# One transpose for both key blocks of a sliding-window attention, and its scaling as one operation a step later

## The chip, the cores and the metric

The kernel runs on one core of a Trainium2 chip. The metric is the device time of one launch in microseconds, of the one core that takes part. Engines: TensorE (PE) multiplies and transposes into PSUM; VectorE (DVE) and ScalarE (ACT) read and write SBUF and PSUM; GpSimd (POOL) works on SBUF; SyncE (SP) issues loads. Each engine works its own queue in order.

## The reference, cut to what matters

Two decoder layers for a prompt of 1024 tokens and a group of 8 samples: layer 0 mixes tokens by gated linear attention, layer 1 by attention over a sliding window, each followed by a squared-ReLU MLP. The change lies in the prompt's attention of layer 1:

```python
def sink_probs(scores, mask, sinks):
    s = jnp.where(mask, scores, -jnp.inf)
    sk = sinks.astype(jnp.float32).reshape(SWA_KV_HEADS, SWA_GROUP)[:, :, None, None]
    m = jnp.maximum(jnp.max(s, axis=-1, keepdims=True), sk)
    p = jnp.exp(s - m)
    return p / (jnp.sum(p, axis=-1, keepdims=True) + jnp.exp(sk - m))

def swa_attend_prompt(q, k, v, sinks):          # 8 blocks of 128 queries
    kk, vv = with_prev(k), with_prev(v)         # keys of the block before, and of the block
    scores = jnp.einsum('bnqkgd,bnskd->bnkgqs', qb, kk).astype(jnp.float32) * (SWA_HEAD_DIM ** -0.5)
    diff = SWA_BLOCK + i - j                    # i: query 0..127, j: key 0..255
    mask = (diff >= 0) & (diff <= SWA_WINDOW) & (key_pos >= 0)
    p = sink_probs(scores, mask[None, :, None, None], sinks)
    o = jnp.einsum('bnkgqs,bnskd->bqnkgd', p.astype(vv.dtype), vv)
```

Window and block are both 128. So query i of a block sees the keys j >= i of the block before and the keys j <= i of its own: the two triangles meet only on the diagonal, where both count. There are 16 query heads of 64 columns over 4 key heads.

## The kernel before

The tokens go in two groups: A is tokens 0 to 511 and the 8 samples, B is tokens 512 to 1023. All linear layers are computed in float32r with a split of each operand into a high and a low part: `split_w` makes `wh` (ACT cast, L201) and `wl` (DVE subtraction, L202) of a weight, `split` the same of an activation (L304, L305), and `mms` issues three matmuls for each tile (L225, L227, L229). The linear layers are cut into jobs, one for each 128 output columns; each job's weights are split while the job before it runs.

The attention is a generator in the background. After each linear job `tick` adds its time to a credit, and while the credit is positive the generator is advanced to its next `yield`, which costs PACE. So attention work of one group is strewn between linear jobs of the other: A's attention beside B's MLP of layer 0, B's beside A's MLP of layer 1. A scheduler then puts each engine's instructions into their final order; `keep_in_program_order` holds an instruction at its place.

`swa_attention` works on 16 units for each group, key head j by query block n, each with 4 query heads (two `m`, two `i`). One step is two halves with a `yield` after each:

- first half: `turn` of unit i-2, which transposes the factors on PE into `ppt` (L1041), once for each key block `kk`, and splits them out of PSUM into `ph` (ACT) and `pl` (DVE); then `softmax` of unit i-1;
- second half: `values` of unit i-2 (L1052, L1053, then `ot`, `of` and a split into the input of the output projection) and `queries` of unit i, a split of `q` into `qs` (ACT L998, L999, DVE L1000, L1001).

`softmax` computes the scores into `psc` (L1012), adds the mask and takes the maximum (L1018, DVE, out of PSUM into `pb`), combines it with the sink (L1022 to L1024), takes the exponential with its sum (ACT, L1026), makes the reciprocal of the whole sum (L1029, L1030), and scales the factors by it with one DVE operation for each head (L1032). This is done for each `m` apart. Units with n = 0 of group A have no block before them (`first`): 4 units with one key block, 28 with two.

Other work on the engines in these stretches: `yf` is the sum of the down projections (DVE, L836, reads PSUM), `hl` the low half of the MLP's hidden values (L305). The rotary embedding `rope`, which runs ahead of each group's attention, is the one place where POOL computes: `qsw` times a sine table (L901), beside a DVE product of the same size (L902).

Of the kernel before, what the change touches and what calls it, by code (L numbers as in the profile page):

```python
# [12 lines left out]
F32 = mybir.dt.float32  # L13
# [7 lines left out]
P = 128  # L21
# [14 lines left out]
PB = 4  # L36
# [32 lines left out]
def tile_hybrid_gla_swa_decoder(  # L69
# [885 lines left out]
    def swa_cache_out(sp, g):  # L955
# [9 lines left out]
    def swa_attention(S, sp, g):  # L965
# [25 lines left out]
        def queries(u):  # L991
# [8 lines left out]
            nc.vector.tensor_tensor(out=qs[dn, 0], in0=q[up], in1=r(qs[up, 0]), op=ALU.subtract)  # L1000
            nc.vector.tensor_tensor(out=qs[up, 1], in0=q[dn], in1=r(qs[dn, 1]), op=ALU.subtract)  # L1001

        def softmax(u):
            kh, kl = keys[u.j]
            k0, n = u.k0, u.n
            u.p = []
            for m in range(2):
# [6 lines left out]
                pb = sp.tile([P, 2, 256], F32, tag="pb", name="pb", bufs=PB)  # L1014
                st = sp.tile([P, 8], F32, tag="st", name="st", bufs=4)
                mx = sp.tile([P, 2], F32, tag="mx", name="mx", bufs=4)
                for i in range(2):
                    nc.vector.tensor_tensor_reduce(out=pb[:, i, k0:], in0=ps[:, i, k0:], in1=S.mask[:, k0:],  # L1018
                                                   scale=1.0, scalar=-3e38, op0=ALU.add, op1=ALU.max,
                                                   accum_out=mx[:, i:i + 1])  # L1020
                sk = S.sink[:, 4 * u.j + 2 * m:4 * u.j + 2 * m + 2]
                nc.vector.tensor_tensor(out=mx, in0=mx, in1=sk, op=ALU.max)  # L1022
                nc.vector.tensor_tensor(out=st[:, 0:2], in0=sk, in1=mx, op=ALU.subtract)
                nc.vector.tensor_scalar_mul(mx, mx, -1.0)  # L1024
                for i in range(2):
                    nc.scalar.activation(out=pb[:, i, k0:], in_=pb[:, i, k0:], func=AF.Exp, bias=mx[:, i:i + 1],  # L1026
                                         accum_out=st[:, 2 + i:3 + i])
                nc.scalar.activation(out=st[:, 0:2], in_=st[:, 0:2], func=AF.Exp)
                nc.vector.tensor_tensor(out=st[:, 4:6], in0=st[:, 0:2], in1=st[:, 2:4], op=ALU.add)  # L1029
                nc.vector.reciprocal(out=st[:, 4:6], in_=st[:, 4:6])  # L1030
                for i in range(2):
                    nc.vector.tensor_scalar_mul(pb[:, i, k0:], pb[:, i, k0:], st[:, 4 + i:5 + i])  # L1032
                u.p.append(pb)
# [435 lines left out]
```

## Time and profile before

| | |
|---|---|
| runs shown | 2276.53, 2277.38, 2277.74 us; median 2277.38 |
| the profiled execution | 2277.55 us, of which the profile's span is 2275.7 |
| PE | busy 2247.7 us, 14612 matmuls and transposes |
| DVE | busy 1470.3 us, 3166 instructions |
| ACT | busy 1218.5 us, 2575 instructions |
| POOL | busy 88.7 us, 133 instructions |
| granted TensorE clock | 0.998 of full speed |
| A's attention, B's attention | first scores at 1044 and 1545, last value products at 1244 and 1780 us |

The span is the time between the first and the last recorded instruction; some 1.85 us of the execution lie around it. A row of the profile gives line, engine and operation, what is written and read, how often, and the mean duration in ns; matmuls are pipelined, so their durations overlap, and what one costs PE is the time from its start to the next start.

### The profile page before, as it was taken

The numbers are of one execution on the slowest core, as the hardware profiler recorded it, in microseconds if no ns is written. First come the engines' busy times: TensorE is split into PE (matmuls) and PEld (weight loads), VectorE is DVE, ScalarE is ACT, GpSimd is POOL, SyncE is SP. The second block draws the span as 40 slices with busy tenths as digits, with TensorE's granted clock in tenths as the row PEclk, the third lists the DMA queues.
The fourth block names the chain that finished last, engine by engine and source line by source line (L and its number), as shares of the span: only waits on it lengthen the run. The fifth ranks groups of instructions, "written<-read, shape, count | busy, mean of one in ns | idle before, by whom it ended". The sixth has DMA issues, their size and how long they took to land.

```text
span 2275.7 us, 39181 instructions
## 1 busy us (share of the span) xinstructions
PE 2247.7 (99%) x14612; PEld 2043.4 (90%) x14612; DVE 1470.3 (65%) x3166; ACT 1218.5 (54%) x2575; POOL 88.7 (4%) x133
## 2 busy tenths in 40 slices
PE   7999999999999999999999999999999999999998
PEld 7998889889999998998888989989999899888886
DVE  5578665676644457666887487658888478544445
ACT  5556644475434445535766456536766456443433
POOL 4010000100000000120000000020000000000000
PEclk9999999999999999999999999999999999999999
DMA  5444322445333335343222354432222354533322
GB/s 169 130 117 118 98 74 77 126 137 157 94 93 90 93 93 170 95 115 88 80 86 78 99 161 135 128 106 85 75 79 76 93 162 127 162 120 93 102 86 77
DMA packets 389183, 247.25 MB, mean 109 GB/s; under 512 B 17816, under 2 KB 368120, under 8 KB 388192
## 3 DMA queue, kind: packets, MB, share of 16 engines
q1 hardware_dynamic: 360736, 196.85, 29.9%
q10 hardware_dynamic: 24000, 25.58, 3.8%
q0 software_dynamic: 4256, 22.31, 2.9%
q8 instruction: 115, 1.88, 0.3%
q14 instruction: 76, 0.62, 0.1%
HBM read 221.19 MB, written 24.25 MB: 108 GB/s over the span
## 4 chain that ended last, share of the span: by engine, by line
PE 92%; DVE 3%; DMA 2%; ACT 1%; issue 1%; ACTq 0%; POOL 0%; DVEq 0%; SPq 0%; POOLq 0%
PE psl L225 25%; PE psl L227 25%; PE psl L229 25%; PE psd L1291 2%; PE psd L1293 2%; PE psd L1292 2%; PE psc L1012 1%; PE ppt L1041 1%; PE pO L727 1%; PE pO L725 1%; PE po L1052 1%; PE po L1053 1%; PE pP L700 1%; DMA wst<-in_swa_w_qkv_dram 0%; DVE wl L202 0%
## 5 line engine op out<-in xcount | busy, mean ns | idle before, releaser
L225 PE MATMUL psl<-xh,wh 128*128 128x512 f32 (+2 forms) x2784 | 890.8, 320 | 0.6 <-ACT sr L554 0.4
L227 PE MATMUL psl<-xl,wh 128*128 128x512 f32 (+2 forms) x2784 | 886.8, 319 | 0.1
L229 PE MATMUL psl<-xh,wl 128*128 128x512 f32 (+2 forms) x2784 | 886.1, 318 | 0.6 <-DVE wl L202 0.5
L201 ACT CAST wh<-wst 128x512 fp32r<-128x512 f32 x656 | 405.4, 620 | 599.6 <-PE psl L227 477.1
L202 DVE TENSOR_TENSOR wl<-wst,wh 128x512 fp32r<-128x512 f32 x656 | 457.8, 700 | 304.1 <-ACT wh L201 282.1
L225 PEld LDWEIGHTS psl<-xh,wh 128*128 128x128 f32 x2784 | 524.2, 188 | 37.1 <-ACT sr L554 0.6
L229 PEld LDWEIGHTS psl<-xh,wl 128*128 128x128 f32 x2784 | 523.6, 188 | 37.5 <-DVE wl L202 1.0
L227 PEld LDWEIGHTS psl<-xl,wh 128*128 128x128 f32 x2784 | 524.2, 188 | 36.4 <-DVE xl L305 0.3
L227 PE MATMUL psl<-hl,wh 128*128 128x256 f32 (+2 forms) x1280 | 390.8, 305 | 0.0
L225 PE MATMUL psl<-hh,wh 128*128 128x256 f32 (+2 forms) x1280 | 390.7, 305 | 0.1
L229 PE MATMUL psl<-hh,wl 128*128 128x256 f32 (+2 forms) x1280 | 390.3, 305 | 0.0
L225 PEld LDWEIGHTS psl<-hh,wh 128*128 128x128 f32 x1280 | 240.9, 188 | 11.3 <-ACT hh L304 0.5
L229 PEld LDWEIGHTS psl<-hh,wl 128*128 128x128 f32 x1280 | 240.9, 188 | 10.7
L227 PEld LDWEIGHTS psl<-hl,wh 128*128 128x128 f32 x1280 | 240.6, 188 | 11.0
L305 DVE TENSOR_TENSOR hl<-rl,hh 128x256 fp32r<-128x256 f32 (+1 forms) x192 | 98.7, 514 | 165.7 <-ACT hh L304 165.1
L836 DVE TENSOR_TENSOR yf<-yf,psl 128x256 f32<-128x256 f32 (+2 forms) x280 | 132.7, 474 | 81.9 <-PE psl L229 79.8
L823 ACT ACTIVATE rl<-psl 128x256 f32<-128x256 f32 (+1 forms) x192 | 87.1, 454 | 93.0 <-PE psl L229 85.2
L1291 PE MATMUL psd<-wls,hh 128*128 128x512 f32 x256 | 101.4, 397 | 0.0
L1293 PE MATMUL psd<-whs,hh 128*128 128x512 f32 x256 | 100.6, 394 | 0.0
L1292 PE MATMUL psd<-wls,hl 128*128 128x512 f32 x256 | 100.5, 393 | 0.0
L824 ACT ACTIVATE rl<-rl 128x256 f32<-128x256 f32 (+1 forms) x192 | 94.5, 492 | 4.5
L304 ACT CAST hh<-rl 128x256 fp32r<-128x256 f32 (+1 forms) x192 | 92.2, 480 | 4.8 <-ACT rl L824 0.7
(327 smaller groups left out, 2348.3 us busy)
## 6 DMA issues: line engine op xcount, KB each, us to landing
wst<-in_ffn_w_up_dram SPq DMA_DIRECT2D x256, 256.0 KB
wst<-in_ffn_w_down_dram SPq DMA_DIRECT2D x256, 256.0 KB
wst<-in_gla_w_in_dram SPq DMA_DIRECT2D x96, 256.0 KB
wst<-in_swa_w_qkv_dram SPq DMA_DIRECT2D x48, 256.0 KB
wst<-in_gla_w_out_dram SPq DMA_DIRECT2D x32, 256.0 KB
wst<-in_swa_w_out_dram SPq DMA_DIRECT2D x32, 256.0 KB
nx<-xs ACTq DMA_DIRECT2D x24, 260.0 KB
xs<-y POOLq DMA_DIRECT2D x2, 2080.0 KB, 8.7
```

The source lines that it names most:

```text
L201: c = nc.scalar.copy(out=wh, in_=st)
L202: s = nc.vector.tensor_tensor(out=wl, in0=st, in1=r(wh), op=ALU.subtract)
L225: nc.tensor.matmul(o, lhsT=wh[:, k % 4, :m], rhs=xh[:, k, c0:c0 + n], start=(k == 0), stop=False)
L227: nc.tensor.matmul(o, lhsT=wh[:, k % 4, :m], rhs=xl[:, k, c0:c0 + n], start=False, stop=False)
L229: nc.tensor.matmul(o, lhsT=wl[:, k % 4, :m], rhs=xh[:, k, c0:c0 + n], start=False, stop=(k == kt - 1))
L304: nc.scalar.copy(out=h, in_=src)
L305: nc.vector.tensor_tensor(out=l, in0=src, in1=r(h), op=ALU.subtract)
L824: nc.scalar.activation(out=rl, in_=rl, func=AF.Square)
L836: nc.vector.tensor_tensor(out=o, in0=o, in1=ps, op=ALU.add)
L1291: nc.tensor.matmul(ps, lhsT=h[:, tok], rhs=wh, start=(k == 0), stop=False)
L1292: nc.tensor.matmul(ps, lhsT=l[:, tok], rhs=wh, start=False, stop=False)
L1293: nc.tensor.matmul(ps, lhsT=h[:, tok], rhs=wl, start=False, stop=(k == HB - 1))
```

## The change

For a unit with two key blocks the factors are transposed together. POOL adds the block before (`a`) onto the block itself (`b_`), and keeps of `a` only its diagonal (a product with the identity). One set of four transposes turns the sum. Then DVE puts the sum's transpose into `a` wherever the key is later than the query (`copy_predicated` with the mask `late`), and subtracts `a` from the sum to get the block's own factors. Both are split from SBUF.

The two `m` of a unit share one `pb` tile and one set of small operations. The scaling is one DVE operation over all four heads; it moves to the start of the next step, ahead of that step's maxima, and is held in program order. The low halves of the queries move from DVE to POOL. Transposes and value products move by half a step.

```diff
-PB = 4
+PB = 2
...
+        S.late = sp.tile([P, P], F32, name="late")
+        nc.gpsimd.dma_start(out=S.late, in_=cmask)
+        nc.vector.tensor_scalar(out=S.late, in0=S.late, scalar1=-1.0, scalar2=1.0, op0=ALU.mult, op1=ALU.add)
...
-            nc.vector.tensor_tensor(out=qs[dn, 0], in0=q[up], in1=r(qs[up, 0]), op=ALU.subtract)
-            nc.vector.tensor_tensor(out=qs[up, 1], in0=q[dn], in1=r(qs[dn, 1]), op=ALU.subtract)
+            nc.gpsimd.tensor_tensor(out=qs[dn, 0], in0=q[up], in1=r(qs[up, 0]), op=ALU.subtract)
+            nc.gpsimd.tensor_tensor(out=qs[up, 1], in0=q[dn], in1=r(qs[dn, 1]), op=ALU.subtract)
...
-                nc.vector.tensor_tensor(out=st[:, 4:6], in0=st[:, 0:2], in1=st[:, 2:4], op=ALU.add)
-                nc.vector.reciprocal(out=st[:, 4:6], in_=st[:, 4:6])
-                for i in range(2):
-                    nc.vector.tensor_scalar_mul(pb[:, i, k0:], pb[:, i, k0:], st[:, 4 + i:5 + i])
-                u.p.append(pb)
+            nc.vector.tensor_tensor(out=st[:, 8:12], in0=st[:, 0:4], in1=st[:, 4:8], op=ALU.add)
+            nc.vector.reciprocal(out=st[:, 8:12], in_=st[:, 8:12])
+            u.st = st
+            if u.first:
+                return
+            a, b_ = (pb4[:, :, :, c:c + P] for c in (0, P))
+            nc.gpsimd.tensor_tensor(out=b_, in0=b_, in1=a, op=ALU.add)
+            nc.gpsimd.tensor_tensor(out=a, in0=a, in1=ident.unsqueeze(1).unsqueeze(1).to_broadcast([P, 2, 2, P]),
+                                    op=ALU.mult)
+
+        def scale(u):
+            st = u.st
+            pb = u.p[:, :, :, u.k0:]
+            rs = st[:, 8:12].rearrange("p (m i) -> p i m", m=2).unsqueeze(3)
+            tc.keep_in_program_order(
+                nc.vector.tensor_tensor(out=pb, in0=pb, in1=rs.to_broadcast([P, 2, 2, 256 - u.k0]), op=ALU.mult))
...
-            for kk in ((1,) if u.first else (0, 1)):
-                pt = aux([P, 2, 2, P], "ppt")
-                for i in range(2):
-                    for m in range(2):
-                        nc.tensor.transpose(pt[:, i, m, :], u.p[m][:, i, kk * P:(kk + 1) * P], ident)
...
-                split(ph, pl, pt)
-                u.pt[kk] = ph, pl
+            pt = aux([P, 2, 2, P], "ppt")
+            for i in range(2):
+                for m in range(2):
+                    nc.tensor.transpose(pt[:, i, m, :], u.p[:, i, m, P:], ident)
...
+            if u.first:
+                split(*halves(1), pt)
+                return
+            late = S.late.bitcast(mybir.dt.uint32).unsqueeze(1).unsqueeze(1).to_broadcast([P, 2, 2, P])
+            a, b_ = (u.p[:, :, :, c:c + P] for c in (0, P))
+            nc.vector.copy_predicated(out=a, mask=late, data=pt)
+            nc.vector.tensor_tensor(out=b_, in0=pt, in1=a, op=ALU.subtract)
+            for kk, t in enumerate((a, b_)):
+                split(*halves(kk), t)
...
-        for i in range(nu + 2):
-            if i >= 2:
-                if units[i - 2].n == 0:
-                    prep_v(units[i - 2].j)
-                turn(units[i - 2])
+        for i in range(nu + 3):
+            if 2 <= i < nu + 2:
+                scale(units[i - 2])
             if 1 <= i <= nu:
                 softmax(units[i - 1])
-            yield PACE
-            if i >= 2:
-                values(units[i - 2])
             if i < nu:
                 if units[i].n == 0:
                     prep_k(units[i].j)
                 queries(units[i])
-            yield PACE
+            if i > 0:
+                yield PACE
+            if i >= 3:
+                values(units[i - 3])
+            if 2 <= i < nu + 2:
+                if units[i - 2].n == 0:
+                    prep_v(units[i - 2].j)
+                turn(units[i - 2])
+            if i < nu + 2:
+                yield PACE
```

How the order of the instructions changes, at three places. On PE, in B's attention, a unit's transposes before (`psl` is a linear job's matmul, `psc` are scores):

```order
L229 MATMUL psl<-hh,wl 128x264
L1041 MATMUL ppt<-ident,pb 128x128 x8
L1012 MATMUL psc<-kh,qs 128x256
L1012 MATMUL psc<-kl,qs 128x256
L1012 MATMUL psc<-kh,qs 128x256
```

and in the changed kernel (`po` are the value products of the unit before):

```order
L1082 MATMUL po<-ph,vv 128x512
L1083 MATMUL po<-pl,vv 128x512
L1082 MATMUL po<-ph,vv 128x512
L1083 MATMUL po<-pl,vv 128x512
L1059 MATMUL ppt<-ident,pb 128x128 x4
L225 MATMUL psl<-xh_15333,wh 128x256
```

Eight transposes ahead of the next unit's scores have become four, behind the value products and ahead of a linear job.

On DVE, in B's attention beside up projections, from the maxima to the scaling before:

```order
L1000 TENSOR_TENSOR qs<-q_17248,qs 64x256
L1024 TENSOR_SCALAR mx<-mx 128x2
L1022 TENSOR_TENSOR mx<-mx,sink 128x2
L1001 TENSOR_TENSOR qs<-q_17248,qs 64x256
L1023 TENSOR_TENSOR st<-sink,mx 128x2
L1024 TENSOR_SCALAR mx<-mx 128x2
L1029 TENSOR_TENSOR st<-st 128x2
L1030 RECIPROCAL st<-st 128x2
L1032 TENSOR_SCALAR pb<-pb,st 128x256 x2
L1029 TENSOR_TENSOR st<-st 128x2
L1030 RECIPROCAL st<-st 128x2
L1032 TENSOR_SCALAR pb<-pb,st 128x256 x2
```

and in the changed kernel, from the scaling of the unit before:

```order
L1052 TENSOR_TENSOR pb<-pb,st 128x1024
L1026 TENSOR_TENSOR mx<-mx,sink 128x4
L202 TENSOR_TENSOR wl<-wst,wh 128x512
L1027 TENSOR_TENSOR st<-sink,mx 128x4
L1028 TENSOR_SCALAR mx<-mx 128x4
L1035 TENSOR_TENSOR st<-st 128x4
L1036 RECIPROCAL st<-st 128x4
L305 TENSOR_TENSOR hl<-rl,hh 128x256
L202 TENSOR_TENSOR wl<-wst,wh 128x512 x2
L1072 COPY_PREDICATED pb<-late,ppt 128x4x128
L1089 TENSOR_TENSOR of<-po,ot 64x256
L305 TENSOR_TENSOR hl<-rl,hh 128x264
```

The queries' subtractions have left the queue, the sum L1035 stands right behind the negated maximum L1028, and the scaling is ahead of both.

On POOL, at the end of B's attention, before:

```order
L901 TENSOR_TENSOR qsw_17240<-qsw_17240,sin 128x512
L901 TENSOR_TENSOR qsw_17241<-qsw_17241,sin 128x512
L1251 DMA gain_23998<-in_norm_ffn_post_dram 128x512
L1251 DMA gain_24000<-in_norm_ffn_post_dram 128x512
L405 DMA xs_90<-y_21464 128x4096
```

and in the changed kernel:

```order
L1004 TENSOR_TENSOR qs<-q_17047,qs 64x256
L1005 TENSOR_TENSOR qs<-q_17047,qs 64x256
L1043 TENSOR_TENSOR pb<-pb 128x4x128
L1044 TENSOR_TENSOR pb<-pb,ident 128x4x128
L1286 DMA gain_23589<-in_norm_ffn_post_dram 128x512
L1004 TENSOR_TENSOR qs<-q_17047,qs 64x256
L1005 TENSOR_TENSOR qs<-q_17047,qs 64x256
L1286 DMA gain_23591<-in_norm_ffn_post_dram 128x512
```

Where POOL had only loads to issue it now has four operations for each unit, and loads stand between them.

## Rows read from the trace of the kernel before

**Rows 1.** The page: PE's busy time, and the chain that ended last.

```profile
PE 2247.7 (99%) x14612; PEld 2043.4 (90%) x14612; DVE 1470.3 (65%) x3166; ACT 1218.5 (54%) x2575; POOL 88.7 (4%) x133
...
PE 92%; DVE 3%; DMA 2%; ACT 1%; issue 1%; ACTq 0%; POOL 0%; DVEq 0%; SPq 0%; POOLq 0%
```

**Rows 2.** Windows, the two attention stretches: busy us of each engine, clock, DMA.

```profile
1044.00:1252.00 208.00, 207.50 (x1060) 174.84 (x1059) 172.55 (x567) 144.39 (x380) 3.65 (x6) 1.00 0.28 81
...
1560.00:1790.00 230.00, 230.00 (x1837) 225.54 (x1836) 188.18 (x605) 155.24 (x425) 1.12 (x2) 1.00 0.27 80
```

**Rows 3.** Timeline of PE, start and us: a unit's eight transposes, another's four.

```profile
1601.84 0.29 PE L229 MATMUL psl<-hh,wl 128*128 128x264 f32 x1
1601.97 1.03 PE L1041 MATMUL ppt<-ident,pb 128*128 128x128 f32 x8
1602.76 0.37 PE L1012 MATMUL psc<-kh,qs 128*128 128x256 f32 x1
...
1105.01 0.60 PE L1041 MATMUL ppt<-ident,pb 128*128 128x128 f32 x4
1105.36 0.36 PE L1012 MATMUL psc<-kh,qs 128*128 128x256 f32 x1
```

**Rows 4.** Groups by shape, DVE, 1044 to 1252 us: busy us, mean ns, idle before.

```profile
L202 DVE TENSOR_TENSOR wl<-wst,wh 128x512 fp32r<-128x512 f32 x60 | 41.1, 685 | 13.6 <-ACT wh L201 10.2 <-PE ppt L1041 3.3
...
L305 DVE TENSOR_TENSOR pl<-ppt,ph 128x512 fp32r<-128x512 f32 x28 | 18.5, 685 | 0.9 <-ACT ph L304 0.8
L1032 DVE TENSOR_SCALAR pb<-pb,st 128x256 f32<-128x256 f32 x48 | 14.7, 348 | 0.6
...
L305 DVE TENSOR_TENSOR xl<-of,xh 128x256 fp32r<-128x256 f32 x16 | 6.7, 418 | 1.4 <-ACT xh L304 1.4
...
L1000 DVE TENSOR_TENSOR qs<-q,qs 64x256 fp32r<-64x256 f32 x14 | 5.9, 419 | 0.4
...
L1023 DVE TENSOR_TENSOR st<-sink,mx 128x2 f32<-128x2 f32 x32 | 5.0, 156 | 0.2
...
L1032 DVE TENSOR_SCALAR pb<-pb,st 128x128 f32<-128x128 f32 x16 | 3.9, 283 | 0.3
```

**Rows 5.** Line L678, a predicated copy out of PSUM in layer 0: ns min/median/max.

```profile
L678 DVE COPY_PREDICATED att_sb<-cm,patt x8: 734/743/749, 106.6 to 391.9; 128x512 f32<-128x512 uint32 x8
```

**Rows 6.** Timeline of POOL in B's rotary embedding.

```profile
1513.33 1.29 POOL L901 TENSOR_TENSOR qsw<-qsw,sin 128x512 f32<-128x512 f32 x1 [4.77 <-DMA qsw<-q]
...
1545.94 1.29 POOL L901 TENSOR_TENSOR qsw<-qsw,sin 128x512 f32<-128x512 f32 x1 [4.44 <-DMA qsw<-q]
```

**Rows 7.** Timeline of DVE at the same times.

```profile
1512.02 0.69 DVE L202 TENSOR_TENSOR wl<-wst,wh 128x512 fp32r<-128x512 f32 x1 [1.52 <-ACT wh L201]
1513.43 1.74 DVE L202 TENSOR_TENSOR wl<-wst,wh 128x512 fp32r<-128x512 f32 x1 [0.71 <-ACT wh L201]
1515.09 0.68 DVE L902 TENSOR_TENSOR q<-q,cos 128x512 f32<-128x512 f32 x1
...
1545.96 0.43 DVE L836 TENSOR_TENSOR yf<-yf,psl 128x264 f32<-128x264 f32 x1 [1.03 <-PE psl L229]
1546.31 1.47 DVE L902 TENSOR_TENSOR q<-q,cos 128x512 f32<-128x512 f32 x1
```

**Rows 8.** Groups in B's rotary stretch, 1486 to 1550 us: POOL, then DVE by shape.

```profile
L901 POOL TENSOR_TENSOR qsw<-qsw,sin 128x512 f32<-128x512 f32 x9 | 11.9, 1322 | 41.2 <-DMA qsw<-q 30.0 <-DVE wl L202 7.1 <-DMA qsw<-kr 4.2
...
L202 DVE TENSOR_TENSOR wl<-wst,wh 128x512 fp32r<-128x512 f32 x22 | 19.6, 890 | 22.5 <-ACT wh L201 21.7 <-DMA qsw<-q 0.8
L902 DVE TENSOR_TENSOR q<-q,cos 128x512 f32<-128x512 f32 x8 | 8.3, 1041 | 0.0
```

**Rows 9.** Groups by shape, 1560 to 1790 us: ACT's exponentials, DVE's `hl`.

```profile
L1026 ACT ACTIVATE pb<-pb,mx 128x256 f32<-128x256 f32 x60 | 29.9, 499 | 2.1 <-DVE mx L1024 1.9
...
L305 DVE TENSOR_TENSOR hl<-rl,hh 128x256 fp32r<-128x256 f32 x16 | 6.8, 423 | 11.4 <-ACT hh L304 11.4
```

**Rows 10.** Tile `po`, whole run: what follows the value products, ns min/median/max.

```profile
L1057 ACT COPY ot<-po x32: 368/369/373, 1064.1 to 1781.1; 64x256 f32<-64x256 f32 x32
```

More of the change, by code (lines that the diff above doesn't have):

```diff
@@ L1013, in softmax @@
                                          start=(kx is kh), stop=(kx is kl))
-                pb = sp.tile([P, 2, 256], F32, tag="pb", name="pb", bufs=PB)
-                st = sp.tile([P, 8], F32, tag="st", name="st", bufs=4)
-                mx = sp.tile([P, 2], F32, tag="mx", name="mx", bufs=4)
                 for i in range(2):
-                    nc.vector.tensor_tensor_reduce(out=pb[:, i, k0:], in0=ps[:, i, k0:], in1=S.mask[:, k0:],
+                    nc.vector.tensor_tensor_reduce(out=pb4[:, i, m, k0:], in0=ps[:, i, k0:], in1=S.mask[:, k0:],
@@ L1028, in softmax @@
[L1028 to L1033 removed]
+                                                   accum_out=mx[:, 2 * m + i:2 * m + i + 1])
@@ new lines, in softmax @@
+            sk = S.sink[:, 4 * u.j:4 * u.j + 4]
+            nc.vector.tensor_tensor(out=mx, in0=mx, in1=sk, op=ALU.max)
+            nc.vector.tensor_tensor(out=st[:, 0:4], in0=sk, in1=mx, op=ALU.subtract)
+            nc.vector.tensor_scalar_mul(mx, mx, -1.0)
+            for m in range(2):
+                for i in range(2):
+                    h = 2 * m + i
+                    nc.scalar.activation(out=pb4[:, i, m, k0:], in_=pb4[:, i, m, k0:], func=AF.Exp,
+                                         bias=mx[:, h:h + 1], accum_out=st[:, 4 + h:5 + h])
@@ new lines, in softmax @@
+            nc.scalar.activation(out=st[:, 0:4], in_=st[:, 0:4], func=AF.Exp)
+            nc.vector.tensor_tensor(out=st[:, 8:12], in0=st[:, 0:4], in1=st[:, 4:8], op=ALU.add)
[7 more added lines that the diff above has]
+                                    op=ALU.mult)
@@ L1035, in turn, with halves @@
+        def scale(u):
[4 more added lines that the diff above has]
+                nc.vector.tensor_tensor(out=pb, in0=pb, in1=rs.to_broadcast([P, 2, 2, 256 - u.k0]), op=ALU.mult))
         def turn(u):
             u.pt = {}
-            for kk in ((1,) if u.first else (0, 1)):
-                pt = aux([P, 2, 2, P], "ppt")
-                for i in range(2):
-                    for m in range(2):
-                        nc.tensor.transpose(pt[:, i, m, :], u.p[m][:, i, kk * P:(kk + 1) * P], ident)
-                ph = sp.tile([P, 2, 2, P], F32R, tag="ph", name="ph", bufs=PT)
-                pl = sp.tile([P, 2, 2, P], F32R, tag="pl", name="pl", bufs=PT)
-                split(ph, pl, pt)
-                u.pt[kk] = ph, pl
+            pt = aux([P, 2, 2, P], "ppt")
+            for i in range(2):
+                for m in range(2):
+                    nc.tensor.transpose(pt[:, i, m, :], u.p[:, i, m, P:], ident)
+            def halves(kk):
+                u.pt[kk] = (sp.tile([P, 2, 2, P], F32R, tag="ph", name="ph", bufs=PT),
+                            sp.tile([P, 2, 2, P], F32R, tag="pl", name="pl", bufs=PT))
+                return u.pt[kk]
+            if u.first:
[7 more added lines that the diff above has]
+                split(*halves(kk), t)
@@ L1102, in swa_samples @@
                 nc.tensor.transpose(pt[:, m, :], t[:, m, :], ident)
-            row = sp.tile([NS, 256], F32, tag="pb", name="srow", bufs=PB)
+            row = sp.tile([P, D], F32, tag="pb", name="srow", bufs=PB)[:NS, :256]
             nc.vector.tensor_copy(out=row, in_=pt.rearrange("p m d -> p (m d)"))
```

16 lines of the change are left out of this document (6 added, 10 removed).

## The prediction

> **What bounds the kernel now.** I read the chain that ended last first. It lies on TensorE (PE) for 92% of the span, and PE is busy 99% of it [rows 1]: time is gained only where PE gets less to do, and lost only where PE is made to wait. Then the windows over the two stretches in which the attention runs beside the linear layers. In group A's stretch PE is busy 207.50 of 208 us, in group B's 230.00 of 230; VectorE (DVE) is busy 172.55 and 188.18 us, so it idles 35.5 and 41.8; ScalarE (ACT) idles 64 and 75; GpSimd (POOL) does almost nothing [rows 2]. Seen over the whole run DVE is at 65%, but here it is at 82 to 83%, and it makes the low halves of the weights (`wl`) that PE needs next. So the question is what the change does to PE's queue, and whether DVE still keeps up.
>
> **PE.** A unit that has two key blocks turns eight 128x128 tiles, in one piece; the next matmul starts 0.79 us after the first transpose. A unit with one block turns four, and the next matmul starts after 0.35 us [rows 3]. A recorded transpose lasts longer than its share of this because transposes overlap, so I count from start to start. The change turns four tiles in every unit: 0.79 - 0.35 = 0.44 us less in each of 28 units (12 in A, 16 in B), 12.3 us. By eighths of 0.79 it would be 0.395 x 28 = 11.1 us; I take the middle, 11.7. The scores, the value products and the linear jobs keep their number. In the new order the four transposes follow the value products of the unit before, half a step after the scaling; nothing there is late, since a step takes 208/16 = 13 us in A, and half a step holds a whole linear job.
>
> **DVE.** Removed in both groups: the scalings, 112 of 348 ns and 16 of 283 ns [rows 4], 43.5 us; of 320 small operations on factors (five lines, 64 each) one half, 160 x 0.156 us, 25.0 us (one of the five lines stands in [rows 4]); the low halves of the queries, 64 x 0.42 us, 26.9 us, which go to POOL. Added: one scaling over 128x1024 in 28 units. The trace has no such row; 128x256 takes 0.418 us and 128x512 0.685 [rows 4], another 512 columns add 0.53, so 1.22 us; two separate 128x512 would be 1.37 us, four separate 128x256 1.67, and these are the upper bounds. Four units scale 128x512, 0.69 each. Then 28 predicated copies at 743 ns [rows 5] and 28 subtractions out of PSUM at 685 ns. The splits into `ph` and `pl` stay 60, and now read SBUF: 685 ns from PSUM, 685 for `wl` from SBUF [rows 4]. That makes 12.6 us less for A (47.1 out, 34.5 in) and 5.8 less for B (48.2 out, 42.4 in). PE's stretches shrink too, by 5.0 and 6.7 us. By these terms DVE would idle 43.1 us in A and 40.9 in B, slightly more in A and slightly less in B than now: the moved work would fit.
>
> **POOL, and what it does to DVE.** POOL gets two 128x512 operations in 28 units and two 64x256 in all 32. Its rotary product over 128x512 takes 1.28 us undisturbed [rows 6]; the half-wide one has no row, I take half, 0.64, between that and 1.28. That is 24 x 1.28 + 32 x 0.64 = 51.2 us in A and 32 x 1.28 + 32 x 0.64 = 61.4 in B, some 4 us in a step of 13 to 15: POOL itself has time. But the trace shows what such an operation costs DVE. At 1513.33 POOL starts its product, DVE starts a `wl` 0.10 us later, and this one takes 1.74 us in place of 0.69. At 1545.94 POOL starts again: the DVE operation that reads PSUM beside it takes its usual 0.43 us, and the next, with two operands in SBUF, 1.47 in place of 0.68 [rows 6, 7]. Over B's rotary stretch 22 `wl` take 890 ns instead of 688 and eight products 1041 instead of 690: 4.4 + 2.8 = 7.2 us lost by DVE over nine POOL operations of 11.9 us, a share of 0.61 [rows 8]. The Trainium skill states the rule behind it (SBUF — State Buffer, section "SBUF: two separate sides"): DVE and GpSimd hold a shared port pair by an exclusive lock for a whole instruction, and a DVE operation with two SBUF inputs falls under it against a GpSimd operation that reads SBUF. The rows here agree (1.74 against 0.69), and by that rule this change pays for each operation that it moves to POOL.
>
> In the changed kernel the operations on DVE with both operands in SBUF are `wl`, `hl`, `pl`, `xl`, the scaling and the small ones, about half of DVE's time; the maxima, `of`, `yf` and the new subtraction read PSUM. So I keep the share of 0.61, with 0 and 1 as its ends: DVE loses 31 us in A and 37.5 in B. That leaves it 11.9 us idle in A and 3.4 in B.
>
> One more wait is added. The sum for the reciprocals stands right behind the negated maxima in DVE's queue wherever a step runs beside an up projection, and it waits for four exponentials of 499 ns, 2.0 us; `hl`, `wl` and the predicated copy stand behind it. For about eight units of B that is up to 16 us; DVE idles 11.4 us ahead of the `hl` of such steps already, waiting for ACT [rows 9], and the new wait falls into the same time. So I charge 4.6 us (ends 0 and 16). B then lacks 4.6 - 3.4 = 1.2 us, which PE waits; A lacks nothing.
>
> **The ends.** The values now come half a step later, so the last unit's run into the output projection. From the last value product its path is two ACT copies, two DVE additions and a cast, about 2 us with 0.37 us for a copy [rows 10] and 0.42 for an operation over 64x256 [rows 4]; in A the order puts 18 short matmuls ahead of the first that needs the result, 18 x 0.13 = 2.3 us [rows 3]. I charge 0.5 us (ends 0 and 4). The mask's load and its one DVE operation run in the linear layers before, where DVE has idle time: nothing. POOL's loads for B's rotary tables and the gains now stand behind attention work on POOL; the tables are issued within A's attention, before 1252, and first used in the stretch from 1486 on [rows 8]: nothing. Halving the `pb` buffers (each twice as wide) costs nothing while a unit's splits end before the next but one's maxima, which the queue orders anyhow.
>
> **The sum.** Against the profiled execution's own time, 2277.55 us (span 2275.7 and 1.85 around it): 2277.55 - 11.7 + 1.2 + 0.5 = 2267.55. The median of the runs shown is 2277.38, 0.17 lower; I say 2267.4 us.
>
> **The rivals.** What decides is the share s of POOL's time that DVE loses. With 43.1 and 40.9 - 4.6 = 36.3 us of idle time PE waits max(0, 51.2 s - 43.1) + max(0, 61.4 s - 36.3) + 0.5.
>
> - *DVE becomes the bound, slower.* The place is the step: the add on POOL starts as the exponentials end, just when DVE's sum (two SBUF operands) is due, and the multiplication follows at once, so two of four POOL operations may hold DVE for their whole 1.28 us. At s = 0.85 PE waits 0.4 + 15.9 + 0.5 = 16.8 us and the result is 5.1 us slower, 2282; at s = 1 it is 8.1 + 25.1 + 0.5 = 33.7 us, 2299. For it speaks that DVE is busier here than in the rotary stretch, against it the PSUM readers. It needs s above 0.85. Chance 0.22.
> - *The gain is given back, no change.* The same with s from 0.70 to 0.85: PE waits 7.2 to 16.8 us, 2273 to 2282. Chance 0.20.
> - *The transposes were hidden anyway*, or their slots fill with other waits of the new order: 2277. PE's idle time of 0.5 us in 438 speaks against it. Chance 0.03.
>
> **How the numbers follow.** My forecast holds for s up to 0.70; its own range is 2265 (no loss) to 2272.8. Chance 0.55. A measurement tells apart about 0.2%, 4.6 us: faster 0.55, same 0.20 + 0.03 = 0.23, slower 0.22. The range begins at 2264.5 (12.3 us of PE, no loss) and goes on to 2286, which is s = 0.88; beyond lies some 0.15, below 0.03.
>
> **What would show it.** Right: four transposes for each unit with 0.35 us slots; DVE's rows for two SBUF operands longer (a mean `wl` of 0.8 to 0.9 us in the attention), those from PSUM unchanged; PE's idle time in the two stretches below 3 us. Wrong: PE idle by 8 us or more with `wl`, `hl` or `ph` as its releaser, DVE busy to the end of each step, or transposes that wait for the scaling. A `wl` that keeps 0.69 us would refute the price of POOL, and then the result is 2265 or 2266.

## The result and the profile after

The changed kernel takes 2308.8 us (median of 4 runs, 2306.72 to 2311.48) against 2277.45 us for the kernel before, measured with it: a ratio of 1.0139, 95% interval 1.0124 to 1.0154. It is 31.4 us slower, where 10 us less had been forecast.

The page of the changed kernel, busy times and the chain that ended last:

```profile
PE 2248.8 (98%) x14500; PEld 2037.7 (88%) x14500; DVE 1504.7 (65%) x2903; ACT 1215.5 (53%) x2543; POOL 224.7 (10%) x254
...
PE 79%; DVE 11%; ACT 3%; DMA 3%; issue 3%; ACTq 0%; POOL 0%; DVEq 0%; SPq 0%; POOLq 0%
```

Against [rows 1] the 112 transposes are gone, but PE is busy 1.1 us longer, DVE 34 us longer and POOL 136 us longer, and DVE's part of the chain has risen from 3% to 11%. The profiled execution's span is 2305.3 us, so PE idles 56.5 us of it, against 2275.7 - 2247.7 = 28.0 before. The waits of PE in B's attention (1540 to 1820 us); each row gives the us in total, the number of waits, and the longest:

```profile
PE psl L225 <- DVE yf L836: 16.6, 8, 3.6
PE psl L225 <- ACT rl L823: 3.3, 2, 1.6
PE ppt L1059 <- DVE st L1027: 2.9, 1, 2.9
PE psc L1019 <- DVE kl L984: 1.2, 1, 1.2
```

In A's attention (1020 to 1262 us) there are three groups with 5.7 us together:

```profile
PE ppt L1059 <- DVE pb L1052: 2.9, 2, 1.5
PE ppt L1059 <- DVE mx L1026: 1.6, 1, 1.6
PE psl L229 <- DVE wl L202: 1.2, 1, 1.2
```

Most of what PE lost, then, lies in B, in eight waits for `yf`: the down projection's matmuls wait until DVE has read the PSUM buffer that they are to write. Before, PE did not wait from 1560 to 1790 us [rows 2], and only once, 0.8 us for `kl`, from 1540 to 1820.

Windows of the changed kernel in B; the columns are those of [rows 2] (PE, PEld, DVE, ACT, POOL busy us, then the clock):

```profile
1560.00:1810.00 250.00, 227.21 (x1758) 220.64 (x1757) 215.74 (x482) 153.22 (x405) 66.37 (x60) 0.97 0.24 70
...
1620.00:1640.00 20.00, 20.00 (x167) 19.78 (x166) 17.29 (x40) 16.04 (x43) 4.22 (x5) 1.00 0.19 54
1640.00:1660.00 20.00, 14.78 (x104) 14.00 (x104) 16.46 (x39) 11.78 (x30) 5.62 (x6) 0.91 0.23 66
...
1656.00:1657.00 1.00, 1.00 (x7) 1.00 (x7) 1.00 (x2) 0.65 (x1) 0.00 (x0) 0.50 0.40 115
...
1760.00:1780.00 20.00, 17.05 (x140) 16.63 (x139) 17.45 (x42) 14.32 (x38) 3.02 (x3) 1.00 0.23 66
```

Two things stand here. PE lacks 23 us of 250 while DVE still idles 34: DVE is late without being full. And the loss comes in lumps: one window of 20 us is full, the next lacks 5.2 us. B has five waits of about 2.9 us or more. In four of the five windows of 20 us that hold them the granted clock is 0.91 on the mean; in the fifth, 1760 to 1780, it is 1.00. Inside, it is 1.00 or 0.50: from 1655.0 to 1658.3 us, which begins 1.5 us after PE has come out of two waits, it is 0.50 (1.2 of 2.4 GHz), and matmuls of 256 columns start 0.21 us apart instead of 0.12. Windows of 1 us show four such stretches in B, from about 1566, 1590, 1655 and 1716 us, each at one of these four waits. That cost is seen in the busy time too: the same 14500 matmuls keep PE busy 2248.8 us here and 2237.9 us in the kernel before with 112 transposes left out (below):

```profile
PE 2237.9 (99%) x14500; PEld 2032.2 (90%) x14500; DVE 1468.0 (65%) x3166; ACT 1221.0 (54%) x2575; POOL 89.2 (4%) x133
```

So the 29.6 us between the two spans are: 9.8 less PE work (2247.7 - 2237.9), 10.9 more busy time for the same work, 28.5 more idle time. Of the 10.9 us the four stretches at 0.50 account for some 8, an estimate: half of PE's busy time in them. The rest is not located; the kernel with a small pair (below) is 3.9 us above 2237.9 too (2241.8), and none of its 1 us windows in the two attention stretches lies below 0.97.

Groups of DVE in B by shape, 1570 to 1810 us (busy us, mean ns, idle before):

```profile
L202 DVE TENSOR_TENSOR wl<-wst,wh 128x512 fp32r<-128x512 f32 x63 | 52.4, 840 | 3.6 <-ACT wh L201 3.1
L305 DVE TENSOR_TENSOR pl<-pb,ph 128x512 fp32r<-128x512 f32 x32 | 23.2, 743 | 0.4 <-ACT ph L304 0.4
L1052 DVE TENSOR_TENSOR pb<-pb,st 128x1024 f32<-128x1024 f32 x15 | 21.5, 1434 | 0.0
...
L836 DVE TENSOR_TENSOR yf<-yf,psl 128x256 f32<-128x256 f32 x32 | 13.2, 413 | 1.4 <-PE psl L229 1.4
L305 DVE TENSOR_TENSOR hl<-rl,hh 128x256 fp32r<-128x256 f32 x15 | 12.0, 802 | 2.6 <-ACT hh L304 2.6
L1072 DVE COPY_PREDICATED pb<-late,ppt 128x512 f32<-128x512 uint32 x15 | 11.0, 735 | 0.3
L1073 DVE TENSOR_TENSOR pb<-ppt,pb 128x512 f32<-128x512 f32 x15 | 10.3, 687 | 0.3
...
L1035 DVE TENSOR_TENSOR st<-st 128x4 f32<-128x4 f32 x14 | 7.1, 509 | 14.7 <-ACT pb L1032 14.6
```

Operations with both operands in SBUF are longer: `wl` 840 ns for 685 [rows 4], `hl` 802 for 423 [rows 9], the sum over 128x4 509 ns on the mean where a small operation took 156 [rows 4]. Those that read PSUM (L836, L1072, L1073) have their usual length. POOL in the same window:

```profile
L1044 POOL TENSOR_TENSOR pb<-pb,ident 128x512 f32<-128x512 f32 x15 | 22.1, 1470 | 1.2
...
L1005 POOL TENSOR_TENSOR qs<-q,qs 64x256 fp32r<-64x256 f32 x12 | 9.3, 776 | 0.9
L1004 POOL TENSOR_TENSOR qs<-q,qs 64x256 fp32r<-64x256 f32 x12 | 8.8, 731 | 74.0 <-ACT qs L1002 74.0
```

One of the lumps in order of time. DVE, from the sum to the `yf` that PE waits for (start, us, operation):

```profile
1645.79 0.16 DVE L1035 TENSOR_TENSOR st<-st 128x4 f32<-128x4 f32 x1 [2.15 <-ACT pb L1032]
...
1646.09 1.36 DVE L305 TENSOR_TENSOR hl<-rl,hh 128x256 fp32r<-128x256 f32 x1
1647.37 2.36 DVE L202 TENSOR_TENSOR wl<-wst,wh 128x512 fp32r<-128x512 f32 x2
1649.65 0.71 DVE L1072 COPY_PREDICATED pb<-late,ppt 128x512 f32<-128x512 uint32 x1
...
1652.41 0.69 DVE L305 TENSOR_TENSOR pl<-pb,ph 128x512 fp32r<-128x512 f32 x1
1653.02 0.41 DVE L836 TENSOR_TENSOR yf<-yf,psl 128x256 f32<-128x256 f32 x1
```

POOL and PE at the same time:

```profile
1645.89 1.27 POOL L1043 TENSOR_TENSOR pb<-pb 128x512 f32<-128x512 f32 x1 [4.28 <-issue]
1647.24 1.34 POOL L1044 TENSOR_TENSOR pb<-pb,ident 128x512 f32<-128x512 f32 x1
```

```profile
1647.98 0.38 PE L225 MATMUL psl<-hh,wh 128*128 128x256 f32 x1 [1.63 <-ACT rl L823]
...
1653.48 0.39 PE L225 MATMUL psl<-hh,wh 128*128 128x264 f32 x1 [3.59 <-DVE yf L836]
```

The exponentials end, DVE's sum and POOL's sum start together, and while POOL makes its pair, `hl` takes 1.36 us and two `wl` 2.36 (0.43 and 1.29 at the same place with memsets, below). Behind them stand the copy, two additions, an `hl`, the subtraction, `xl` and a split, 3.4 us in all, and only then `yf`. PE stands still twice, 5.2 us together.

When a held operation ends is seen on the sum, where it comes shortly after POOL's addition: at 1614.91 us L1035 starts 0.31 us after L1043 (1614.60, for 1.28 us), takes 0.99 us in place of 0.16, and ends with it, within 0.02 us.

### The profile page after: what moved, and what is told of

Same layout as the page of the kernel before. It is cut to its first block, busy times and chain, and to the rows that moved or that the text cites. A ratio compares the mean times of both kernels' runs of the same rounds, so it can differ in the third digit from the quotient of the medians.

```text
span 2305.3 us, 38859 instructions
## 1 busy us (share of the span) xinstructions
PE 2248.8 (98%) x14500; PEld 2037.7 (88%) x14500; DVE 1504.7 (65%) x2903; ACT 1215.5 (53%) x2543; POOL 224.7 (10%) x254
## 3 DMA queue, kind: packets, MB, share of 16 engines
q1 hardware_dynamic: 360736, 196.85, 29.6%
## 4 chain that ended last, share of the span: by engine, by line
PE 79%; DVE 11%; ACT 3%; DMA 3%; issue 3%; ACTq 0%; POOL 0%; DVEq 0%; SPq 0%; POOLq 0%
PE psl L225 22%; PE psl L227 22%; PE psl L229 22%; PE psd L1326 2%; PE psd L1328 2%; PE psd L1327 2%; DVE wl L202 2%; DVE pb L1052 1%; ACT pb L1032 1%; DVE pb L1022 1%; DMA wst<-in_ffn_w_up_dram 1%; PE psc L1019 1%; ACT wh L201 1%; DVE pl L305 1%; DVE hl L305 1%
## 5 line engine op out<-in xcount | busy, mean ns | idle before, releaser
L202 DVE TENSOR_TENSOR wl<-wst,wh 128x512 fp32r<-128x512 f32 x656 | 474.5, 727 | 290.7 <-ACT wh L201 275.7
L225 PE MATMUL psl<-hh,wh 128*128 128x256 f32 (+2 forms) x1280 | 395.5, 309 | 20.6 <-DVE yf L836 16.6
L305 DVE TENSOR_TENSOR hl<-rl,hh 128x256 fp32r<-128x256 f32 (+1 forms) x192 | 107.2, 558 | 150.9 <-ACT hh L304 150.2
L836 DVE TENSOR_TENSOR yf<-yf,psl 128x256 f32<-128x256 f32 (+2 forms) x280 | 131.8, 473 | 77.5 <-PE psl L229 76.5
```

What stands on the lines that cost most here:

```text
L202: s = nc.vector.tensor_tensor(out=wl, in0=st, in1=r(wh), op=ALU.subtract)
L225: nc.tensor.matmul(o, lhsT=wh[:, k % 4, :m], rhs=xh[:, k, c0:c0 + n], start=(k == 0), stop=False)
L305: nc.vector.tensor_tensor(out=l, in0=src, in1=r(h), op=ALU.subtract)
L836: nc.vector.tensor_tensor(out=o, in0=o, in1=ps, op=ALU.add)
```

## The experiments

Two theories at the start. **L**: POOL's pair holds DVE's operations with two SBUF operands, just where PE is about to need their results. **Q**: the sum, which waits for the exponentials in DVE's queue, holds up what is behind it. Ratios are to the kernel before, measured beside each run. Differences between two changed kernels are differences of their medians.

### The pair cut to 16 columns

```diff
-            nc.gpsimd.tensor_tensor(out=b_, in0=b_, in1=a, op=ALU.add)
-            nc.gpsimd.tensor_tensor(out=a, in0=a, in1=ident.unsqueeze(1).unsqueeze(1).to_broadcast([P, 2, 2, P]), op=ALU.mult)
+            nc.gpsimd.tensor_tensor(out=b_[:, :, :, 0:4], in0=b_[:, :, :, 0:4], in1=a[:, :, :, 0:4], op=ALU.add)
+            nc.gpsimd.tensor_tensor(out=a[:, :, :, 0:4], in0=a[:, :, :, 0:4], in1=ident[:, 0:4].unsqueeze(1).unsqueeze(1).to_broadcast([P, 2, 2, 4]), op=ALU.mult)
```

> The changed kernel with its two POOL operations for each unit (the add of the block before, the product with the identity) cut from 512 to 16 columns, so the block before is mostly left out of the sum; the order on PE, DVE and ACT stays as it was. Theory L (POOL holds DVE): the pair holds `wl`, `hl`, `pl`, the sum and the scaling, and what PE loses comes from that; without it PE waits fall from 30 us to under 10 and the time is 2266 to 2280 us. Theory Q (DVE's queue: the sum for the reciprocals waits about 2 us for four exponentials, and `hl` and `yf` stand behind it): that wait stays, and the time stays within 8 us of the changed kernel's 2308.8, above 2300.

Measured 2277.2 us, ratio 1.0000 (0.9991 to 1.0009). The full width of the pair is worth 2308.8 - 2277.2 = 31.6 us: L. PE's waits for `yf` in B fall from 16.6 to 5.8 us, and DVE is busy 1472.5 us instead of 1504.7. But this is still not 2266.

### The sum moved behind the exponentials' step

```diff
-            nc.vector.tensor_tensor(out=st[:, 8:12], in0=st[:, 0:4], in1=st[:, 4:8], op=ALU.add)
-            nc.vector.reciprocal(out=st[:, 8:12], in_=st[:, 8:12])
...
         def scale(u):
             st = u.st
+            tc.keep_in_program_order(nc.vector.tensor_tensor(out=st[:, 8:12], in0=st[:, 0:4], in1=st[:, 4:8], op=ALU.add))
+            tc.keep_in_program_order(nc.vector.reciprocal(out=st[:, 8:12], in_=st[:, 8:12]))
```

> The changed kernel with the sum for the reciprocals and the reciprocals taken out of the softmax and put right ahead of the scaling, a step later, pinned with it. DVE then waits for no exponential. Theory Q: DVE's waits for ACT behind the negated maxima (26 us over both groups in the changed kernel) go, PE no longer waits for `yf` and `hl`, and the time falls to 2268 to 2285 us. Theory L: POOL holds DVE as long as before, and the time stays above 2298.

Measured 2306.97 us, ratio 1.0129 (1.0114 to 1.0144): 1.8 us less than the changed kernel, while four runs of each scatter over 3 to 5 us. PE's waits for `yf` in B stay:

```profile
PE psl L225 <- DVE yf L836: 17.4, 9, 3.6
```

Q explains next to nothing.

### Both together

The two edits above in one kernel.

> Both edits of the two other runs: the sum and the reciprocals a step later, and the POOL pair cut to 16 columns (the block before mostly left out of the sum). Both theories: PE waits under 3 us, so that only the removed transposes show: 2264 to 2270 us. Above 2275 a third cause is at work (the moved transposes and values, the maxima of all four heads ahead of the first exponential).

Measured 2278.08 us, ratio 1.0001 (0.9991 to 1.0010). With the pair small, moving the sum brings nothing either, and some 11 us stay that neither theory has. The expectation failed; a third cause had to be looked for.

### The kernel before with 112 transposes left out

```diff
-            for kk in ((1,) if u.first else (0, 1)):
-                pt = aux([P, 2, 2, P], "ppt")
...
+            for kk in ((1,) if u.first else (1, 0)):
+                if kk == 1 or u.first:
+                    pt = aux([P, 2, 2, P], "ppt")
...
```

> The kernel before with the transposes of the block before left out (both splits read the one transposed block, so the value products are those of the wrong factors); everything else is as before. It prices the 112 removed transposes by themselves: 2277.4 - 11.7 = 2265.7 us (2265 to 2267) if each four cost PE 0.40 to 0.44 us; 2277 if they were hidden; 2247 if each cost its recorded duration of 0.27 us.

Measured 2266.15 us, ratio 0.9950 (0.9934 to 0.9967): 10.7 us less than the kernel before measured beside it (2276.82), 11.7 had been worked out. The transposes were not hidden. This is the mark that the changed kernel should have come near.

### Is it the hold, or the wait for the pair's data?

With a small pair two things vanish at once: POOL's work, and the time until its data are there. Two runs part them. Behind the small pair POOL does full-width work on query blocks that nothing reads any more; PE, DVE and ACT keep exactly the order of the kernel with the small pair.

```diff
+            d = g.q[:, 2 * u.j:2 * u.j + 2, (u.n - 1) * P:(u.n + 1) * P]
...
+            tc.keep_in_program_order(nc.gpsimd.tensor_tensor(out=d, in0=d, in1=d, op=ALU.add))
+            tc.keep_in_program_order(nc.gpsimd.tensor_tensor(out=d, in0=d, in1=ident.unsqueeze(1).unsqueeze(1).to_broadcast([P, 2, 2, P]), op=ALU.mult))
```

> The kernel with the small POOL pair (16 columns instead of 512, 2277.2 us), and behind each small pair two full-width POOL operations of the same shape and kind on a tile that nothing reads any more (query blocks already used), in 27 units. They are held in order on POOL only; PE, DVE and ACT keep the very same order, and no result waits for them. Leaves out what the small pair leaves out. Theory L (a POOL operation holds DVE's operations with two SBUF operands): the 31.6 us come back although nobody waits for the data, 2277 + 27/28 x 31.6 = about 2307, at least 2298. Theory D (the pair cost time because scaling, transposes and sum waited for POOL's data): 2277, within 2 us. Between 2283 and 2295 both have a part.

The other has memsets in place of the two operations:

```diff
+            for _ in range(4):
+                tc.keep_in_program_order(nc.gpsimd.memset(d, 0.0))
```

> The same as the run with the idle full-width pair, with four POOL memsets over 128x512 in place of its two operations: POOL is about as long at work, but reads nothing; the trace of the kernel before has a POOL memset over 128x640 at 0.64 us, so four over 512 columns are some 2.1 us against 2.6. Theory L in its narrow form (it is POOL's reads from SBUF that hold DVE): 2277 to 2281, wl at its usual 0.7 us. In a wide form (any POOL operation on SBUF holds DVE): 2277 + 2.1/2.6 x 30 = about 2301. Theory D: 2277.

Measured 2308.38 us (ratio 1.0142, 1.0127 to 1.0157) with the idle pair, and 2276.39 us (0.9999, 0.9990 to 1.0009) with the memsets. The idle pair gives the changed kernel's time to within 0.5 us although no result waits for it, and in B it is again eight waits for `yf` that make up most of PE's waiting. PE's waits in B (1570 to 1810 us) with the idle pair (in these two kernels the lines from L836 on are numbered 570 higher):

```profile
PE psl L225 <- DVE yf L1406: 19.1, 8, 4.2
PE psl L225 <- ACT rl L1393: 1.9, 3, 0.8
```

With the memsets:

```profile
PE psl L225 <- DVE yf L1406: 5.7, 4, 2.1
```

Groups in the same window with the idle pair, DVE and POOL:

```profile
L202 DVE TENSOR_TENSOR wl<-wst,wh 128x512 fp32r<-128x512 f32 x62 | 56.8, 924 | 3.0 <-ACT wh L201 1.8
...
L1625 POOL TENSOR_TENSOR q<-q,ident 128x512 f32<-128x512 f32 x15 | 23.4, 1558 | 1.2
L1624 POOL TENSOR_TENSOR q<-q 128x512 f32<-128x512 f32 x15 | 16.0, 1069 | 0.0
```

With the memsets:

```profile
L202 DVE TENSOR_TENSOR wl<-wst,wh 128x512 fp32r<-128x512 f32 x70 | 47.6, 688 | 17.6 <-ACT wh L201 16.5
...
L1624 POOL MEMSET q<- 128x512 f32 x56 | 29.4, 526 | 2.4
```

The four memsets of a unit keep POOL busy 2.1 us (4 x 526 ns), the idle pair 2.6, but they read nothing, and `wl` keeps its 688 ns; with operands that POOL reads from SBUF, `wl` takes 924. The idle pair starts behind the small one, some 0.7 us later than the changed kernel's pair, so here it is `wl` that is held, while `hl` over 256 columns (423 ns) and the sum (171) keep their length. Here is the same place of the program as in the lump above, with the memsets, DVE:

```profile
1631.51 0.43 DVE L305 TENSOR_TENSOR hl<-rl,hh 128x256 fp32r<-128x256 f32 x1
1632.03 1.29 DVE L202 TENSOR_TENSOR wl<-wst,wh 128x512 fp32r<-128x512 f32 x2
...
1636.83 0.41 DVE L1406 TENSOR_TENSOR yf<-yf,psl 128x256 f32<-128x256 f32 x1
```

From the start of `hl` to that of `yf` it is 5.32 us, against 6.93 in the changed kernel, and PE waits 1.64 us once instead of 1.63 and 3.59. So L is shown, and in its narrow form: the hold comes from POOL's reads. The Trainium skill (SBUF — State Buffer, section "SBUF: two separate sides") says just this of a DVE operation with two SBUF inputs, that it takes the shared ports only against a GpSimd operation that reads SBUF. The two runs agree (924 against 688 ns).

### What keeps the last 11 us

Two edits of the kernel with the small pair. The queries' low halves back on DVE:

```diff
-            nc.gpsimd.tensor_tensor(out=qs[dn, 0], in0=q[up], in1=r(qs[up, 0]), op=ALU.subtract)
-            nc.gpsimd.tensor_tensor(out=qs[up, 1], in0=q[dn], in1=r(qs[dn, 1]), op=ALU.subtract)
+            nc.vector.tensor_tensor(out=qs[dn, 0], in0=q[up], in1=r(qs[up, 0]), op=ALU.subtract)
+            nc.vector.tensor_tensor(out=qs[up, 1], in0=q[dn], in1=r(qs[dn, 1]), op=ALU.subtract)
```

> The kernel with the small POOL pair (2277.2 us) and the queries' low halves back on DVE, so that POOL does nothing of weight in the attention. It still lies 11 us above the kernel before with 112 transposes left out (2266.2). If the queries' low halves on POOL are what keeps these 11 us: 2266 to 2270. If it is the new order on DVE (the sum of the down projection, yf, standing behind the copy, the subtraction and the splits of a unit): 2277 or more, since DVE gets 0.42 us x 2 more in each unit; up to 2285.

The step in three parts:

```diff
             if i > 0:
-                yield PACE
+                yield PACE * 2 / 3
             if i >= 3:
                 values(units[i - 3])
+                yield PACE * 2 / 3
             if 2 <= i < nu + 2:
...
                 turn(units[i - 2])
             if i < nu + 2:
-                yield PACE
+                yield PACE * 2 / 3
```

> The kernel with the small POOL pair (2277.2 us), with its step cut in three parts instead of two: scaling, scores and queries; values; transposes and what follows them; each a third of the step's time. So the value products' additions and the transposes' copy, subtraction and splits no longer come on DVE in one piece ahead of yf: in the order, the last hl of an up projection and the first yf behind it now have 'mx of st of mx' between them, where 'of pb xl pl' stood. Theory R (that piece makes PE wait for yf, 5.8 us in four waits, and the clock falls after them): 2266 to 2271 and waits for yf below 1 us. If the piece only moves and makes PE wait elsewhere, or the 11 us have another cause: 2275 to 2282.

The two edits in one kernel:

> The kernel with the small pair (2277.2 us), with both edits that each took something off: the queries' low halves on DVE (2273.8, 3.4 less) and the step in three parts (2273.45, 3.75 less). If these are two separate causes, their sum: 2277.2 - 7.2 = 2270, 4 us above the kernel before with 112 transposes left out (2266.2). If both only take the same waits for yf away: 2273.

Measured 2273.8 us (ratio 0.9988, 0.9979 to 0.9998), 2273.45 us (0.9987, 0.9978 to 0.9997), and with both 2268.93 us (0.9965, 0.9952 to 0.9978). Alone, each gives less than its theory had promised; together they take 8.3 of the 11 us, about the sum of 3.4 and 3.75: by the intervals each of the medians is known to some 2 us, so the two sizes are rough. PE's waits in B (1540 to 1820 us), with the small pair alone:

```profile
PE psl L225 <- DVE yf L836: 5.8, 4, 2.1
...
PE ppt L1059 <- DVE st L1027: 0.8, 1, 0.8
```

With both edits:

```profile
PE psl L225 <- DVE yf L836: 1.0, 3, 0.5
PE ppt L1059 <- DVE st L1035: 0.7, 1, 0.7
...
```

With the queries on DVE alone the waits for `yf` are 3.1 us, with three parts alone 2.9, where below 1 had been expected. So POOL's small work, two operations over 64x256 in a unit, costs 3.4 to 4.5 us, and the lump of value additions and turned splits that the new order put ahead of `yf` costs 3.75 to 4.9 us. The cut into three parts moves more than this lump; that the lump itself is the cause is read from the waits for `yf`, not tried by itself. The last 2.8 us above 2266.15 stay open.

### Is there a version that is faster than both?

If POOL must not read SBUF here, the pair has to go elsewhere. First onto DVE, behind the scaling:

```diff
-            nc.gpsimd.tensor_tensor(out=b_, in0=b_, in1=a, op=ALU.add)
...
+            if not u.first:
+                a, b_ = (u.p[:, :, :, c:c + P] for c in (0, P))
+                nc.vector.tensor_tensor(out=b_, in0=b_, in1=a, op=ALU.add)
+                nc.vector.tensor_tensor(out=a, in0=a, in1=ident.unsqueeze(1).unsqueeze(1).to_broadcast([P, 2, 2, P]), op=ALU.mult)
```

> The changed kernel with the sum and the diagonal's product on DVE, right behind the scaling (a step behind the scores), in place of POOL. DVE gets 28 x 2 x 0.685 = 38 us more to do of its own, 16.4 in A and 21.9 in B, about what it lost to POOL's pair in the changed kernel (some 15 in A and 28 in B by the longer rows), but at a place where it waits for nothing, and never in the middle of wl or hl. If what counts is only how much of DVE's time goes: 2277 + 38/43 x 31.6 = 2305. If what counts is where it goes (the hold falls on the sum, hl and wl at the end of the exponentials): 2277 to 2290. Below 2274 would beat the kernel before.

The same in three parts:

> The run before this one (the pair on DVE behind the scaling) with the step cut in three parts (scaling, scores, queries; values; transposes and splits), which took 3.7 us off the kernel with the small pair. If the lump of DVE work ahead of yf costs as much here: 3 to 5 us below the kernel with the pair on DVE. If DVE's load sets the time: the same as it, within 2 us.

Measured 2289.84 us (ratio 1.0055, 1.0040 to 1.0070) and 2282.6 us (1.0024, 1.0014 to 1.0034). The first lies at the upper end of the range given for "where it goes". The second is 7.2 us below the first, more than the 3 to 5 of its expectation. The page of the first, busy times:

```profile
PE 2246.5 (98%) x14500; PEld 2035.4 (89%) x14500; DVE 1501.9 (66%) x2959; ACT 1214.0 (53%) x2543; POOL 152.0 (7%) x198
```

DVE is busy 1501.9 us, within 3 of the changed kernel, yet the kernel is 19 us faster. The same amount of DVE time is cheaper as work of its own at the start of a step than as holds of `hl` and `wl`; but it is not free.

Last, the pair on DVE at the start of the step, the scaling on ACT in its place, the queries on DVE, and the step in three parts:

```diff
         def scale(u):
...
-                nc.vector.tensor_tensor(out=pb, in0=pb, in1=rs.to_broadcast([P, 2, 2, 256 - u.k0]), op=ALU.mult))
+            if not u.first:
+                a, b_ = (u.p[:, :, :, c:c + P] for c in (0, P))
+                tc.keep_in_program_order(nc.vector.tensor_tensor(out=b_, in0=b_, in1=a, op=ALU.add))
+                tc.keep_in_program_order(nc.vector.tensor_tensor(out=a, in0=a, in1=ident.unsqueeze(1).unsqueeze(1).to_broadcast([P, 2, 2, P]), op=ALU.mult))
+            for m in range(2):
+                for i in range(2):
+                    h = 8 + 2 * m + i
+                    nc.scalar.activation(out=u.p[:, i, m, u.k0:], in_=u.p[:, i, m, u.k0:], func=AF.Copy, scale=u.st[:, h:h + 1])
...
```

> A version made of what the runs before showed: sum and diagonal's product on DVE at the start of the step (never on POOL), the scaling on ACT as four operations of a head each, the queries' low halves on DVE, the step in three parts. POOL has no work in the attention that reads SBUF. Against the run with thirds, the small pair and the queries on DVE (2268.9) DVE gets 28 x 1.37 = 38 us more and 28 x 1.22 = 34 us less; ACT gets 28 x 4 x some 0.4 us = 45 us more, of the 139 us that it idles in the two stretches. If PE's waits come from POOL's holds and DVE's lumps alone: 2268 to 2272, below the kernel before. If ACT's queue now delays rl, hh or wh: 2275 to 2285. This run computes the whole reference.

Measured 2273.9 us, ratio 0.9985 (0.9976 to 0.9995): 2.9 us faster than the kernel before and 35 us faster than the changed kernel. It is slower than the 2268 to 2272 of the expectation's first case. Of the 11 us that the transposes give back, 3 are kept. Its page and PE's waits in B:

```profile
PE 2240.7 (99%) x14500; PEld 2032.5 (89%) x14500; DVE 1483.2 (65%) x2991; ACT 1260.6 (55%) x2671; POOL 89.8 (4%) x134
```

```profile
PE ppt L1057 <- ACT pb L1049: 1.7, 4, 0.6
PE psc L1019 <- DVE kl L984: 1.5, 1, 1.5
PE psl L225 <- DVE yf L836: 1.4, 2, 1.0
```

ACT has 45 us more to do, as worked out, and is late only for the transposes, by 1.7 us in B and 0.5 in A.

## Why the prediction was wrong

- **PE's term was right.** The prediction took 11.7 us for 28 units' transposes; leaving them out of the kernel before gives 10.7 (11.3 against the median of 2277.45).
- **DVE's own work was right.** The sum was 12.6 + 5.8 = 18.4 us less. In the run with both edits POOL has almost no work, and DVE is busy 1481.2 us; without 26.9 us for the queries that is 1454.3, 16.0 below the 1470.3 of before. The new operations cost what the prediction took for them: 735 and 687 ns in the rows above for 743 and 685, and a scaling beside which POOL does nothing took 1.22 us (at 1639.40 us of the run with memsets), as forecast; the mean of 1434 ns in B has the holds in it.
- **POOL's own time was too low**: 136 us more against 112.6 forecast. An operation over 64x256 took 0.73 to 0.78 us on the mean in B and 0.91 to 1.07 in A, not half of 1.28; one over 128x512 took 1.29 to 1.47.
- **The share s was not too low.** Against those 1454.3 us DVE lost 1504.7 - 1454.3 = 50.4 us to 136 us of POOL's work, a share of 0.37. The prediction took 0.61, and 0.85 as the point from which the kernel would be slower.
- **The step that failed** is the rule by which that share became time: "With 43.1 and 40.9 - 4.6 = 36.3 us of idle time PE waits max(0, 51.2 s - 43.1) + max(0, 61.4 s - 36.3) + 0.5." With the share of 0.37 it gives half a microsecond; the pair cost 31.6 us. Idle time of DVE over a whole stretch is no reserve for an operation that PE waits for. DVE kept 34 us of idle time in B while PE waited 24, because POOL's pair starts as the exponentials end and holds what stands there. In six of B's 16 units that is `hl` (1.36 to 1.38 us) and two `wl` (2.36 to 2.39), one behind the other. In three of these (from 1582, 1646 and 1710 us) the `yf` that frees PE's PSUM buffer stands a few microseconds behind, and PE waits 3.2 to 3.6 us for it; in the other three (from 1630, 1694 and 1757 us) an up projection comes next, and PE does not wait. The idle time comes at other places of the step. And four of the five longest waits in B were paid twice, with a stretch at half the clock: some 8 us by the estimate above, which the prediction had at nothing.
- **The signs named ahead** were half right: `wl` rose to 0.84 us in B and the reads of PSUM kept their length, as told; but in B, where most was lost, PE's releasers became `yf` and `rl`, which the list of bad signs (`wl`, `hl`, `ph`, transposes that wait for the scaling) did not name. `hl` was late, and PE felt it one and two operations further on. In A two of the named signs did come: the transposes waited 2.9 us for the scaling (2.9 with the idle pair too, so not for POOL's data), and PE waited 1.2 us for `wl`. B's one wait of the transposes, 2.9 us, ended with the small operation (L1027) right behind a scaling.
- **The rival on the other side had the place, not the mechanism.** It named the add that starts with the end of the exponentials, and with 2282 to 2299 even came near in size. But it asked for a DVE with no time left (s above 0.85), and so it got a chance of 0.22. The time lost was a matter of where the held operations stand.
- **The wait for the exponentials** was charged with 4.6 us (ends 0 and 16); taking it away gave 1.8 us with the full pair and nothing with the small one.
- **The moved half step** was held to cost nothing ("nothing there is late"). That looked at PE's order only. On DVE it put the values' additions and the turned splits together, ahead of `yf`: 3.75 to 4.9 us by the run in three parts.
- **The queries on POOL** were counted as 26.9 us off DVE. Moving them back made DVE busier by only 1484.0 - 1472.5 = 11.5 us, and the kernel 3.4 us faster: more than half of what they spared DVE came back as holds.

The sum by runs: 2277.45, less 11.3 for the transposes (2266.15), 2.8 open (2268.93), 8.3 for the queries on POOL and the order of the step (2277.2), 31.6 for the pair (2308.8).

## What to carry to other kernels

Before moving an operation with SBUF operands to GpSimd, look at what VectorE does at that moment: an operation with both operands in SBUF that starts while GpSimd reads SBUF is held until GpSimd's ends, and what this costs is set by who waits for the held operation, not by VectorE's idle time. Two cheap runs tell it: shrink the operation to a few columns, then put an operation of full width on dead data beside it. Where TensorE is the bound, cost a long wait with the slower clock that can follow it, and compare at the turns of the step which reads of PSUM now stand behind a lump of other work.

## What the runs showed of the hardware

- A POOL memset over 128x512 (526 ns, 108 of them) cost the kernel nothing, where the 54 operations of the idle pair, which read SBUF and take 1.04 to 1.56 us each, cost 31 us.
- Of the changed kernel's 32 sums over 128x4 (L1035), 11 took 0.88 to 1.28 us and the others 0.15 to 0.17. The 11 started 0.03 to 0.81 us after POOL's addition and ended with it, to within 0.03 us: a hold does not depend on how small the held operation is, but on how long POOL's still runs.
- POOL's own operations got longer too: its product over 128x512 took 1470 ns on average in B, 1.29 us undisturbed [rows 6]. That DVE holds POOL in turn is likely by this, but was not tried.
